# Value products of latent attention: three of nine key tiles and the value factors in fp32 instead of fp32r parts

## The chip, the cores and the metric

One core of a Trainium2 chip runs the whole kernel. The metric is device time in microseconds; the figure of a kernel is the median of its runs. The profile is of one execution of its own.

## The reference, cut to what matters

Two layers of a diffusion backbone run over 1024 latent tokens and 128 context ("prompt") tokens of width 1024. Layer 0 is multi-head latent attention with 16 heads, layer 1 a neighbourhood attention. The change is in layer 0:

```
c_kv   = rms_norm(kv_a, kv_norm_g)                       # keys x 128, shared by the heads
k_nope, v = split(c_kv @ w_kvb)                          # per head: 128 + 128
s = (q_nope @ k_nope.T + q_rope @ k_rope.T) * MLA_SCALE  # all 1024 + 128 cached context keys
o = softmax(s) @ v
y = (o * silu(gate)) @ w_out
```

The kernel doesn't form v for the latent queries. It computes (softmax(s) @ c_kv) @ w_v: a value product over the 9 key tiles of 128 keys in the latent space (tile 0 is the cached context, tiles 1 to 8 the latent tokens), and then one product with the head's 128 x 128 value factor w_v. The prompt's queries go the same way over their own 128 keys (tile 9).

## The kernel before

Precision: an fp32 operand x is split into a high part hi = fp32r(x), written by ScalarE as a copy, and a low part lo = fp32r(x - hi), written by VectorE or GpSimd (`split_to`, lines 147 to 149). A product is then three fp32r matmuls, hi*hi, hi*lo and lo*hi (`mm3`, lines 84 to 87, PASSES).

Stages: modulation, first norm, gates and narrow projections (to about 350 us); 64 units of latent attention (350 to 1203 us), a unit being one head and 256 queries; the output projection of layer 0 (to about 1500 us); layer 1.

In the attention the instructions of TensorE, ScalarE, VectorE and GpSimd are issued in an order written out by hand: ORDERS has eight strings, one for each unit modulo 8, and each engine works through its own instructions in that order. While unit `un` is finished, the scores of the next one, `nx`, are made, and the unit before, `f`, is closed. The steps:

- s0 to s4 (`scores`, line 741): scores of `nx`, two key tiles to a PSUM bank, 36 matmuls. m0 to m4 (`run_max`, lines 749 to 758): the running maximum, on ScalarE and VectorE.
- e0 to e4 (`exp`, line 799): exp of a bank of `un` to the fp32 tile `pf` (512 columns, the last 256: two key tiles of 256 queries). +1 to +4 (`sums`, lines 817 to 822): GpSimd adds the `pf` tiles up.
- h0 to h4 (`hi`, line 804, ScalarE) and l0 to l4 (`lo`, line 809, VectorE): the two parts of `pf` for the value products.
- v01, v26, v78 (`values`, line 828, booked on line 87): the value products of key tiles 0 to 1, 2 to 6 and 7 to 8, three matmuls each, summed in the bank `pso`. V (`values_out`): the result goes to `ol` as two parts, a ScalarE copy and a VectorE subtraction.
- L0 to L5 (lines 839 to 850): transpose of the sums, reciprocal, back to a row. M0 to M5 (lines 763 to 786): the same for the maxima of `nx`; M5 puts the row of maxima where X (`last_scores`, line 792) adds it to the scores in their banks. Only then can the exps of `nx` begin.
- F (`finish`, lines 854 and 856): row sums to all partitions, and the product of `ol` with the head's value factor `wv`. O (`finish_out`): gate and store.
- H takes the next of the weights' splits, P and p start a product of the next heads' queries or of the prompt (`do_prod`), ES and EV evacuate it, A runs one of its later steps, T lets it go on. The prompt's chain for two heads is in `prompt_work`; its steps `latent` and `val` are its two value products.

Banks: tag M has two PSUM banks, which `psv` (F), `pso` (first v) and `pm` (L0 and M0) take in turn. `pf` has NPF = 5 buffers, each part of it NPT = 5. The head's raw weights come by one DMA from SP's queue (`load_head`); `split_v` splits the value factor at the second unit of the head before.

```
if c == "v":
    n = step[1:]
    values(un, range(int(n[0]), int(n[-1]) + 1))
```

Of the kernel before, what the change touches and what calls it, by code (L numbers as in the profile page):

```python
# [11 lines left out]
F32 = mybir.dt.float32  # L12
# [21 lines left out]
EPS = 1e-6  # L34
GW = 64
ORDERS = [
# [8 lines left out]
]  # L45
NPF = 5
NPT = 5
NORDER = "K A0 K A1 J1 C0 Z m0 K J2 X1 W R C1 m1 X1 K K K J2 h0 x0 h1 J1 r0 l0 E R x1 l1 n0 K r1 R f n1 K K g K K"
PASSES = ((0, 0), (0, 1), (1, 0))
# [7 lines left out]
def hybrid_step(ctx: ExitStack, tc: tile.TileContext, i, o):  # L57
# [302 lines left out]
    V.tensor_copy(onesR, ones)  # L360
    cKT = [ap.tile([P, 10, P], F32R, name=f"cKT{e}") for e in range(2)]
    cK = [ap.tile([P, 10, LAT], F32R, name=f"cK{e}") for e in range(2)]
    KR = [ap.tile([P, 10, P], F32R, name=f"KR{e}") for e in range(2)]
    for j in range(10):
        V.tensor_copy(KR[1][64:66, j, :], ones[64:66, :])
# [24 lines left out]
    def narrow(t):  # L390

        j = t + 1
        ps = bank("W")[:, :NARROW]
        for ko in range(NKO):
            mm3(ps, [hT[e][:, ko, t * P:(t + 1) * P] for e in range(2)], [w448[e][:, ko, :] for e in range(2)],
                ko == 0, ko == NKO - 1)
        pj = p1.tile([P, NARROW], F32, tag="pj", name="pj", bufs=2)
        S.copy(pj, ps)
        ss = p1.tile([P, 2], F32, tag="ss2", name="ss2", bufs=2)
        junk = p1.tile([P, QLR], F32, tag="junk2", name="junk2", bufs=1)  # L400
        S.activation(junk, pj[:, 0:QLR], AF.Square, accum_out=ss[:, 0:1])
        S.activation(junk[:, :LAT], pj[:, QLR:QLR + LAT], AF.Square, accum_out=ss[:, 1:2])
        V.tensor_scalar(ss[:, 0:1], ss[:, 0:1], 1.0 / QLR, EPS, ALU.mult, ALU.add)
        V.tensor_scalar(ss[:, 1:2], ss[:, 1:2], 1.0 / LAT, EPS, ALU.mult, ALU.add)
        r = rsqrt(p1, ss, 2)

        V.tensor_scalar(pj[:, 0:QLR], pj[:, 0:QLR], r[:, 0:1], MLA_SCALE, ALU.mult, ALU.mult)
        cf = p1.tile([P, LAT], F32, tag="cf", name="cf", bufs=2)
        V.scalar_tensor_tensor(cf, pj[:, QLR:QLR + LAT], r[:, 1:2], gkv, ALU.mult, ALU.mult)
        split_to(cK[0][:, j, :], cK[1][:, j, :], cf)  # L410
        kr2 = p1.tile([P, 2, 64], F32, tag="kr2", name="kr2", bufs=2)
        krp = pj[:, QLR + LAT:NARROW]
        if t == 8:
            dma(o["s_ckv"], cf)
            dma(o["s_kr"], krp)
            V.tensor_copy(kr2[:, 0, :], krp)
        else:
            rot = p1.tile([P, 64], F32, tag="rot", name="rot", bufs=2)
            sw = krp.rearrange("p (a b c) -> p a b c", a=2, b=2)
            sv = ropeSk[:, t, :].rearrange("p (a b c) -> p a b c", a=2, b=2)  # L420
            rv = rot.rearrange("p (a b c) -> p a b c", a=2, b=2)
            for b in range(2):
                V.tensor_tensor(rv[:, :, b, :], sw[:, :, 1 - b, :], sv[:, :, b, :], ALU.mult)
            V.tensor_tensor(kr2[:, 0, :], krp, ropeCk[:, t, :], ALU.mult)
            V.tensor_tensor(kr2[:, 0, :], kr2[:, 0, :], rot, ALU.add)
        V.tensor_copy(kr2[:, 1, :], kr2[:, 0, :])
        pt = bank("T")
        nc.tensor.transpose(pt[:, 0:P], pj[:, 0:P], ident)
        nc.tensor.transpose(pt[:, P:2 * P], pj[:, P:2 * P], ident)
        nc.tensor.transpose(pt[:, 2 * P:3 * P], cf, ident)  # L430
        nc.tensor.transpose(pt[:, 3 * P:4 * P], kr2.rearrange("p a b -> p (a b)"), ident)
        qf = p1.tile([P, 2, P], F32, tag="qf", name="qf", bufs=2)
        for c in range(2):
            V.tensor_scalar(qf[:, c, :], pt[:, c * P:(c + 1) * P], gq[:, c:c + 1], None, ALU.mult)
        split_to(qaT[0][:, :, t * P:(t + 1) * P], qaT[1][:, :, t * P:(t + 1) * P], qf)
        split_to(cKT[0][:, j, :], cKT[1][:, j, :], pt[:, 2 * P:3 * P], V)
        put_kr(j, pt[:, 3 * P:4 * P])

    def load_head(h, tile_):

        raw, rr = tile_[:, 0:512], None
        dma(raw, i["whead"][h])
        if h % 2 == 0:
            rr = tile_[:, 512:768]
            dma(rr, i["wr"][h // 2].rearrange("p k c -> p (k c)"))
        return raw, rr
# [12 lines left out]
            split_to(wr[0], wr[1], rr)  # L459
        head_w[h].append(wr)  # L460

    def split_v(h, raw):
        wv = [ap2.tile([P, LAT], F32R, tag=f"wv{e}", name=f"wv{e}", bufs=4) for e in range(2)]
        split_to(wv[0], wv[1], raw[:, 384:512])
        head_wv[h] = wv

    narrow(0)
    for h in range(2, 6):
# [10 lines left out]
    for h in range(6, H - 2):  # L479
        for n, _ in enumerate(gate(h, gate_w(h))):  # L480
            for _ in range(1 + (n == 1)):
                next(rest, None)
        next(rest, None)
        if h == 10:
            raw = load_head(0, pg.tile([P, 1024], F32, tag="raw", name="w_raw", bufs=4))
            split_qk(0, raw[0])
            split_r(0, raw[1])
            split_v(0, raw[0])
    for _ in rest:
        pass  # L490
    es_m.close()
# [125 lines left out]
    def prompt_work(h):  # L617
# [43 lines left out]

        def spl(nm, n):
            def fn():
                c["t"] = [p2.tile([P, 2 * P], F32R, tag=f"{nm}{e}", name=f"{nm}{e}", bufs=1) for e in range(2)]
                split_to(c["t"][0], c["t"][1], c["s"])
                fresh.add((h, n))
            return fn

# [4 lines left out]
        def val():  # L673
            c["gt"] = p2.tile([P, 256], F32, tag="gt", name="gt", bufs=3)
            c["ps"] = bank("W")[:, :2 * P]
            for e in range(2):
                dma(c["gt"][:, e * P:(e + 1) * P], gate_d[h - 1 + e][:, qs])
                mm3(c["ps"][:, e * P:(e + 1) * P], head_wv[h - 1 + e], [x[:, e * P:(e + 1) * P] for x in c["t"]])

        def val_out(eng):  # L680
            og = p2.tile([P, 256], F32, tag="og", name="og", bufs=2)
# [140 lines left out]
            G.tensor_tensor(sm[:, 0:256], sm[:, 0:256], sm[:, 256:512], ALU.add)  # L822

    def values(un, js):
        if js[0] == 0:
            un["pso"] = bank("M")[:, :256]
        for j in js:
            mm3(un["pso"], [cK[e][:, j, :] for e in range(2)],
                [x[:, (j % 2) * 256:(j % 2) * 256 + 256] for x in un["pT"][j // 2]], j == 0, j == 8)

    def values_out(un):
        un["ol"] = [p2.tile([P, 256], F32R, tag=f"ol{e}", name=f"ol{e}", bufs=2) for e in range(2)]
        split_to(*un["ol"], un["pso"], V)

    def sum_cols(un, bank_):
        un["gt"] = load_gate(un["h"], un["qs"])
# [15 lines left out]
    def finish(un):  # L852

        nc.tensor.matmul(un["rs"][:, 0:256], onesR, row, start=True, stop=True)
        un["psv"] = bank("M")[:, :256]
        mm3(un["psv"], un["wv"], un["ol"])

    def finish_out(un):
        gr = p2.tile([P, 256], F32, tag="gr", name="gr", bufs=2)
# [28 lines left out]
    with tc.high_priority(offset=300):  # L888
# [2 lines left out]
        raw = load_head(1, pg.tile([P, 1024], F32, tag="raw", name="w_raw", bufs=4))  # L891
        split_qk(1, raw[0])
        split_r(1, None)
        split_v(1, raw[0])
    for _ in gate(H - 1, w_last, "M"):
        pass

# [98 lines left out]
    for k, (h, u) in enumerate(units):  # L996
# [13 lines left out]
        splits = deque()  # L1010
        if u == 1 and h + 1 < H:
            if h:
                splits.append(lambda: split_v(h + 1, head_raw[h + 1][0]))
            splits.append(lambda: h + 2 < H and head_raw.update({h + 2: load_head(h + 2, new_raw(0))}))
        if u == 2 and h + 2 < H:
            splits.append(lambda: split_qk(h + 2, head_raw[h + 2][0]))
# [942 lines left out]
```

## Time and profile before

| what | value |
|---|---|
| median of 3 runs | 2181.25 us |
| lowest and highest | 2176.08 and 2183.51 us |
| profiled execution, time | 2177.92 us |
| its span in the trace | 2176.1 us |
| mean granted TensorE clock | 0.98 of full speed |
| busy: TensorE, VectorE, ScalarE, GpSimd | 93%, 67%, 51%, 39% |

Times in the trace count from the start of the span. Busy is the share of the span in which an engine executes; matmuls overlap in their pipeline, so the time from start to start of neighbours tells more than the duration of one. In the timeline a row is a run of like instructions: start, length, engine, line, operation, tiles, count, and in brackets how long the engine stood idle before it and for whom. VectorE is DVE, ScalarE ACT, GpSimd POOL there; PEld is TensorE's weight load.

### The profile page before, as it was taken

The numbers are of one execution on the slowest core, as the hardware profiler recorded it, in microseconds if no ns is written. First come the engines' busy times: TensorE is split into PE (matmuls) and PEld (weight loads), VectorE is DVE, ScalarE is ACT, GpSimd is POOL, SyncE is SP. The second block draws the span as 40 slices with busy tenths as digits, with TensorE's granted clock in tenths as the row PEclk, the third lists the DMA queues.
The fourth block names the chain that finished last, engine by engine and source line by source line (L and its number), as shares of the span: only waits on it lengthen the run. The fifth ranks groups of instructions, "written<-read, shape, count | busy, mean of one in ns | idle before, by whom it ended". The sixth has DMA issues, their size and how long they took to land.

```text
span 2176.1 us, 37859 instructions
## 1 busy us (share of the span) xinstructions
PE 2017.5 (93%) x13166; PEld 1861.4 (86%) x13166; DVE 1460.2 (67%) x3224; ACT 1105.3 (51%) x2577; POOL 854.0 (39%) x847
## 2 busy tenths in 40 slices
PE   7899998889989898889898799999999999999898
PEld 3799997888888888888887788889889999999686
DVE  4723877778887888788888645642215778888743
ACT  5545115565556565656565433442214666677631
POOL 1412215676766677767665400010001333333400
PEclk9999999999999999999999999999999999999899
DMA  8223752212121212221211643425424555556753
GB/s 292 93 69 109 228 166 79 59 46 64 46 64 51 66 49 76 61 68 49 60 45 57 222 151 117 136 74 161 163 101 146 178 178 175 172 181 204 216 148 97
DMA packets 174931, 256.49 MB, mean 118 GB/s; under 512 B 20690, under 2 KB 138226, under 8 KB 174740
## 3 DMA queue, kind: packets, MB, share of 16 engines
q1 hardware_dynamic: 174476, 253.71, 37.5%
q8 instruction: 104, 1.70, 0.3%
q14 instruction: 87, 0.71, 0.1%
q10 hardware_dynamic: 136, 0.26, 0.0%
q0 software_dynamic: 128, 0.11, 0.0%
HBM read 182.58 MB, written 51.49 MB: 108 GB/s over the span
## 4 chain that ended last, share of the span: by engine, by line
PE 40%; DVE 4%; ACT 4%; POOL 4%; DMA 3%; issue 2%; SPq 0%; DVEq 0%; POOLq 0%; ACTq 0%
PE ps_S L87 16%; PE ps_W L87 11%; PE ps_M L87 5%; PE ps_M L1675 2%; POOL sm L820 2%; PE ps_T L1650 2%; PE ps_S L1623 1%; PE ps_S L1624 1%; ACT pf L799 1%; DMA vw<-vd 1%; DMA w_raw<-in_wout 1%; DVE rm L754 1%; DVE pT L809 1%; DVE og L82 1%; DMA w_raw<-og_d 1%
## 5 line engine op out<-in xcount | busy, mean ns | idle before, releaser
L809 DVE TENSOR_TENSOR pT<-pf,pT 128x512 fp32r<-128x512 f32 (+1 forms) x320 | 306.9, 963 | 24.2 <-ACT pT L804 24.0
L820 POOL TENSOR_TENSOR sm<-sm,pf 128x512 f32<-128x512 f32 (+1 forms) x192 | 259.5, 1352 | 16.0 <-ACT pf L799 2.0
L87 PE MATMUL ps_M<-pT,cK 128*128 128x256 f32 x1728 | 259.3, 296 | 1.3 <-DVE pT L809 1.3
L87 PE MATMUL ps_W<-h,w 128*128 128x384 f32 x1152 | 237.6, 345 | 0.4 <-DVE w L82 0.4
L87 PEld LDWEIGHTS ps_M<-pT,cK 128*128 128x128 f32 x1728 | 230.8, 198 | 1.9 <-DVE pT L809 1.9
L87 PEld LDWEIGHTS ps_W<-h,w 128*128 128x128 f32 x1152 | 197.9, 188 | 6.4 <-DVE w L82 0.7
L741 PE MATMUL ps_S<-qA,cKT 128*128 128x256 f32 x1152 | 190.1, 285 | 5.6 <-ACT pf L799 5.3
L87 PE MATMUL ps_S<-hT,w_hi 128*128 128x384 f32 x720 | 190.5, 342 | 4.3 <-DVE hT L82 2.6
L804 ACT CAST pT<-pf 128x512 fp32r<-128x512 f32 (+1 forms) x320 | 179.7, 591 | 0.0
L741 PEld LDWEIGHTS ps_S<-qA,cKT 128*128 128x128 f32 x1152 | 166.2, 192 | 8.2 <-ACT pf L799 7.6
L1645 POOL TENSOR_SCALAR pf<-pf,li 128x512 f32<-128x512 f32 x128 | 90.7, 709 | 199.3 <-DVE li L1642 176.7
L87 PEld LDWEIGHTS ps_S<-hT,w_hi 128*128 128x128 f32 x720 | 130.9, 189 | 6.7 <-DVE hT L82 3.3
L817 POOL TENSOR_TENSOR sm<-pf 128x512 f32<-128x512 f32 x64 | 88.8, 1387 | 110.7 <-ACT pf L799 110.4
L87 PE MATMUL ps_S<-wo,og 128*128 128x512 f32 x432 | 124.0, 395 | 0.0
L786 ACT CAST q<-ps_M 2x256 fp32r<-2x256 f32 x63 | 22.7, 360 | 197.3 <-PE ps_M L780 185.1
L87 PE MATMUL ps_S<-hT,w_lo 128*128 128x384 f32 x360 | 121.8, 339 | 0.0
L1639 ACT ACTIVATE pf<-pf,nm 128x512 f32<-128x512 f32 x128 | 93.0, 726 | 34.0 <-DVE nm L1636 30.8
L741 PE MATMUL ps_S<-q,KR 128*128 128x256 f32 x384 | 108.6, 284 | 0.3 <-DMA q<-w_raw 0.3
L799 ACT ACTIVATE pf<-ps_S 128x512 f32<-128x512 f32 x192 | 108.8, 598 | 0.0
L82 DVE TENSOR_TENSOR og<-w_raw,og 128x512 fp32r<-128x512 f32 x56 | 57.0, 1038 | 67.4 <-ACT og L148 54.2
L519 ACT COPY qt<-ps_W 128x384 f32<-128x384 f32 (+1 forms) x104 | 46.9, 451 | 100.3 <-PE ps_W L87 93.2
L741 PE MATMUL ps_T<-qA,cKT 128*128 128x256 f32 x576 | 97.2, 284 | 0.0
(376 smaller groups left out, 5035.4 us busy)
## 6 DMA issues: line engine op xcount, KB each, us to landing
w_raw<-in_w_ada SPq DMA_DIRECT2D x48, 512.0 KB
w_raw<-og_d SPq DMA_DIRECT2D x41, 512.0 KB
vw<-vd SPq DMA_DIRECT2D x128, 128.0 KB
bias<-in_bias SPq DMA_DIRECT2D x64, 192.0 KB
q<-rp SPq DMA_DIRECT2D x126, 96.0 KB
gate_d<-gt SPq DMA_DIRECT2D x48, 192.0 KB
w_raw<-in_wgate SPq DMA_DIRECT2D x16, 512.0 KB
gt<-gate_d SPq DMA_DIRECT2D x64, 128.0 KB
```

What stands on the lines that cost most here:

```text
L82: eng.tensor_tensor(out, a, b, ALU.subtract)
L87: nc.tensor.matmul(ps, lhs[a], rhs[b], start=first and n == 0, stop=last and n == 2)
L519: (eng.copy if eng is S else eng.tensor_copy)(out, src)
L741: nc.tensor.matmul(ps[:, c:c + 256], k_[:, j, :], q_[:, un["qs"]], start=c == 0 and n == 0, stop=n == 3, skip_group_check=True)
L799: S.activation(pf, un["banks"][b][:, :w], AF.Exp)
L804: S.copy(un["pT"][b][0][:, :pf.shape[1]], pf)
L809: V.tensor_tensor(x[1], pf, x[0].bitcast(F32), ALU.subtract)
L817: G.tensor_tensor(un["sm"], un["pf"][0], pf, ALU.add)
L820: G.tensor_tensor(sm[:, :w], sm[:, :w], pf, ALU.add)
L1639: S.activation(it["pf", rg], it["pf", rg], AF.Exp, bias=it["nm", rg], scale=1.0, accum_out=it["li", rg])
L1645: G.tensor_scalar(it["pf", rg], it["pf", rg], it["li", rg][:, 0:1], 1.0, ALU.mult, ALU.mult)
L1650: nc.tensor.transpose(pt[:, j * P:(j + 1) * P], it["pf", rg][:, j * P:(j + 1) * P], ident)
```

## The change

Key tiles 6, 7 and 8 (from WHOLE = 6 on) are kept as plain fp32 in `cKf` and multiplied with the plain `pf` tiles 3 and 4, one fp32 matmul instruction for three fp32r ones. The steps h3, h4, l3 and l4 go from all eight orders. The value products change their order: v68 (fp32) stands first, at or behind the place of v01 and behind e4, then v03 in the place of v26, then v45 in that of v78. The value factor `wv` isn't split: it has a DMA of its own and is multiplied in fp32 with an unsplit `ol`, in F and in the prompt's `val`; `values_out` is one ScalarE copy. The prompt's last split (`spl("tp", 3)`) becomes a ScalarE copy alone.

```diff
 ORDERS = [
...
-    "H e0 F s0 H O e1 T +1 h0 s1 l0 e2 A m0 m1 h1 e3 s2 +2 P +3 s3 l1 m2 h2 l2 h3 e4 ES h4 m3 v01 s4 +4 A A m4 P L0 M0 l3 A A M1 L1 A L2 A M2 p v26 L3 M3 ES L4 w l4 A EV M4 ES A v78 M5 V L5 X",
+    "H e0 F s0 H O e1 T +1 h0 s1 l0 e2 A m0 m1 h1 e3 s2 +2 P +3 s3 l1 m2 h2 l2 e4 ES m3 v68 s4 +4 A A m4 P L0 M0 A A M1 L1 A L2 A M2 p v03 L3 M3 ES L4 w A EV M4 ES A v45 M5 V L5 X",
...
-    "F e0 O H ES s0 H e1 +1 h0 s1 l0 T e2 A m0 e3 m1 s2 p m2 T e4 h1 +2 +3 s3 l1 h2 l2 h3 m3 p +4 s4 m4 v01 h4 ES l3 P M0 P L0 L1 M1 L2 v26 M2 L3 ES A M3 l4 w L4 M4 v78 A M5 L5 X V",
+    "F e0 O H ES s0 H e1 +1 h0 s1 l0 T e2 A m0 e3 m1 s2 p m2 T e4 h1 +2 +3 s3 l1 h2 l2 m3 p +4 s4 m4 v68 ES P M0 P L0 L1 M1 L2 v03 M2 L3 ES A M3 w L4 M4 v45 A M5 L5 X V",
...
 NPF = 5
+WHOLE = 6
...
+    cKf = ap.tile([P, 9 - WHOLE, LAT], F32, name="cKf")
...
-        cf = p1.tile([P, LAT], F32, tag="cf", name="cf", bufs=2)
+        cf = cKf[:, j - WHOLE, :] if WHOLE <= j < 9 else p1.tile([P, LAT], F32, tag="cf", name="cf", bufs=2)
         V.scalar_tensor_tensor(cf, pj[:, QLR:QLR + LAT], r[:, 1:2], gkv, ALU.mult, ALU.mult)
-        split_to(cK[0][:, j, :], cK[1][:, j, :], cf)
+        if not WHOLE <= j < 9:
+            split_to(cK[0][:, j, :], cK[1][:, j, :], cf)
...
-        dma(raw, i["whead"][h])
+        dma(raw[:, 0:384], i["whead"][h][:, 0:384])
...
-    def split_v(h, raw):
-        wv = [ap2.tile([P, LAT], F32R, tag=f"wv{e}", name=f"wv{e}", bufs=4) for e in range(2)]
-        split_to(wv[0], wv[1], raw[:, 384:512])
-        head_wv[h] = wv
+    def load_v(h):
+        head_wv[h] = ap2.tile([P, LAT], F32, tag="wv", name="wv", bufs=4)
+        dma(head_wv[h], i["whead"][h][:, 384:512])
...
-                mm3(c["ps"][:, e * P:(e + 1) * P], head_wv[h - 1 + e], [x[:, e * P:(e + 1) * P] for x in c["t"]])
+                nc.tensor.matmul(c["ps"][:, e * P:(e + 1) * P], head_wv[h - 1 + e],
+                                 c["t"][0][:, e * P:(e + 1) * P].bitcast(F32), start=True, stop=True)
...
     def values(un, js):
-        if js[0] == 0:
+        if js[0] == WHOLE:
             un["pso"] = bank("M")[:, :256]
         for j in js:
-            mm3(un["pso"], [cK[e][:, j, :] for e in range(2)],
-                [x[:, (j % 2) * 256:(j % 2) * 256 + 256] for x in un["pT"][j // 2]], j == 0, j == 8)
+            c = slice((j % 2) * 256, (j % 2) * 256 + 256)
+            if j >= WHOLE:
+                nc.tensor.matmul(un["pso"], cKf[:, j - WHOLE, :], un["pf"][j // 2][:, c], start=j == WHOLE, stop=False)
+            else:
+                mm3(un["pso"], [cK[e][:, j, :] for e in range(2)], [x[:, c] for x in un["pT"][j // 2]], False,
+                    j == WHOLE - 1)
 
     def values_out(un):
-        un["ol"] = [p2.tile([P, 256], F32R, tag=f"ol{e}", name=f"ol{e}", bufs=2) for e in range(2)]
-        split_to(*un["ol"], un["pso"], V)
+        un["ol"] = p2.tile([P, 256], F32, tag="ol", name="ol", bufs=2)
+        S.copy(un["ol"], un["pso"])
...
-        mm3(un["psv"], un["wv"], un["ol"])
+        nc.tensor.matmul(un["psv"], un["wv"], un["ol"], start=True, stop=True)
...
-                splits.append(lambda: split_v(h + 1, head_raw[h + 1][0]))
+                splits.append(lambda: load_v(h + 1))
```

## Rows read from the trace of the kernel before

**Rows 1.** Busy time by engine in the attention's stretch (us, instructions; clock, DMA).

```profile
350.00:1203.00 853.00, 765.93 (x6017) 732.56 (x6017) 697.87 (x1388) 503.08 (x1181) 579.92 (x495) 0.98 0.20 57
```

**Rows 2.** Waits, 350 to 1203 us: total us, times, longest.

```profile
ACT q L786 <- PE ps_M L780: 185.1, 58, 7.7
...
PE ps_M L763 <- DVE rm L758: 37.5, 30, 3.3
PE ps_M L839 <- POOL sm L820: 35.4, 49, 2.1
```

**Rows 3.** Timeline of TensorE: waits at L0 and M0.

```profile
675.88 0.44 PE L839 MATMUL ps_M<-ident,sm 128*128 128x128 f32 x2 [0.84 <-POOL sm L820]
...
700.78 0.44 PE L839 MATMUL ps_M<-ident,sm 128*128 128x128 f32 x2 [0.49 <-POOL sm L820]
701.67 0.44 PE L763 MATMUL ps_M<-ident,rm 128*128 128x128 f32 x2 [0.45 <-DVE rm L758]
...
713.55 0.44 PE L839 MATMUL ps_M<-ident,sm 128*128 128x128 f32 x2 [0.34 <-POOL sm L820]
...
725.75 0.44 PE L839 MATMUL ps_M<-ident,sm 128*128 128x128 f32 x2 [0.47 <-POOL sm L820]
...
740.57 0.44 PE L763 MATMUL ps_M<-ident,rm 128*128 128x128 f32 x2 [1.33 <-DVE rm L758]
...
755.52 0.44 PE L763 MATMUL ps_M<-ident,rm 128*128 128x128 f32 x2 [3.08 <-DVE rm L758]
...
770.10 0.44 PE L763 MATMUL ps_M<-ident,rm 128*128 128x128 f32 x2 [0.69 <-DVE rm L758]
...
545.16 0.44 PE L763 MATMUL ps_M<-ident,rm 128*128 128x128 f32 x2 [1.82 <-DVE rm L758]
```

**Rows 4.** Timeline of TensorE, value products of one unit and their neighbours.

```profile
710.81 0.87 PE L87 MATMUL ps_M<-pT,cK 128*128 128x256 f32 x6
711.52 0.52 PE L741 MATMUL ps_T<-qA,cKT 128*128 128x256 f32 x3
...
713.96 2.04 PE L87 MATMUL ps_M<-pT,cK 128*128 128x256 f32 x15
...
715.85 0.28 PE L780 MATMUL ps_M<-identR,lir 128*2 128x128 f32 x2
```

**Rows 5.** Timeline of line 179, then single tiles: duration in ns (least/median/most), forms.

```profile
25.41 1.88 PE L179 MATMUL ps_S<-w_raw,c 128*4 128x512 f32 x4
27.22 0.63 PE L179 MATMUL ps_S<-w_hi,cs 128*4 128x512 f32 x2
...
L179 PEld LDWEIGHTS ps_S<-w_raw,c x16: 82/86/87, 25.4 to 38.3; 128*4 128x4 f32 x16
...
L190 PEld LDWEIGHTS ps_T<-sel,mod x32: 181/187/187, 23.3 to 42.0; 5*128 5x128 f32 x32
...
L87 PEld LDWEIGHTS ps_M<-pT,cK x1728: 186/188/338, 352.0 to 1199.7; 128*128 128x128 f32 x192
```

**Rows 6.** Groups by line and form, VectorE: count, busy us, mean ns, idle before.

```profile
L809 DVE TENSOR_TENSOR pT<-pf,pT 128x512 fp32r<-128x512 f32 x256 | 279.3, 1096 | 24.2 <-ACT pT L804 24.0
...
L82 DVE TENSOR_TENSOR ol<-ps_M,ol 128x256 fp32r<-128x256 f32 x64 | 27.1, 423 | 78.7 <-ACT ol L148 78.6
```

**Rows 7.** Timeline behind the 3.08 us gap; windows with the granted clock (third from last).

```profile
756.02 3.47 PE L87 MATMUL ps_M<-pT,cK 128*128 128x256 f32 x15
759.33 0.28 PE L780 MATMUL ps_M<-identR,lir 128*2 128x128 f32 x2
...
545.00:549.00 4.00, 3.84 (x34) 3.81 (x35) 3.32 (x13) 1.08 (x4) 1.40 (x2) 1.00 0.00 0
756.00:758.00 2.00, 2.00 (x11) 2.00 (x10) 1.62 (x9) 0.00 (x0) 0.00 (x0) 0.50 0.00 0
```

**Rows 8.** Timeline of VectorE: l3 and the last part of the maxima.

```profile
713.35 0.70 DVE L809 TENSOR_TENSOR pT<-pf,pT 128x512 fp32r<-128x512 f32 x1
...
715.51 0.15 DVE L775 TENSOR_TENSOR nmr<-nm,nmr 128x2 fp32r<-128x2 f32 x1
```

More of the change, by code (lines that the diff above doesn't have):

```diff
@@ L487, in hybrid_step @@
             split_r(0, raw[1])
-            split_v(0, raw[0])
+            load_v(0)
     for _ in rest:
@@ L663, in fn @@
             def fn():
-                c["t"] = [p2.tile([P, 2 * P], F32R, tag=f"{nm}{e}", name=f"{nm}{e}", bufs=1) for e in range(2)]
-                split_to(c["t"][0], c["t"][1], c["s"])
+                c["t"] = [p2.tile([P, 2 * P], F32R, tag=f"{nm}{e}", name=f"{nm}{e}", bufs=1) for e in range(4 - n)]
+                if n == 3:
+                    S.copy(c["t"][0].bitcast(F32), c["s"])
+                else:
+                    split_to(c["t"][0], c["t"][1], c["s"])
                 fresh.add((h, n))
@@ L824, in values @@
     def values(un, js):
-        if js[0] == 0:
+        if js[0] == WHOLE:
             un["pso"] = bank("M")[:, :256]
         for j in js:
-            mm3(un["pso"], [cK[e][:, j, :] for e in range(2)],
-                [x[:, (j % 2) * 256:(j % 2) * 256 + 256] for x in un["pT"][j // 2]], j == 0, j == 8)
+            c = slice((j % 2) * 256, (j % 2) * 256 + 256)
+            if j >= WHOLE:
+                nc.tensor.matmul(un["pso"], cKf[:, j - WHOLE, :], un["pf"][j // 2][:, c], start=j == WHOLE, stop=False)
+            else:
+                mm3(un["pso"], [cK[e][:, j, :] for e in range(2)], [x[:, c] for x in un["pT"][j // 2]], False,
+                    j == WHOLE - 1)
     def values_out(un):
-        un["ol"] = [p2.tile([P, 256], F32R, tag=f"ol{e}", name=f"ol{e}", bufs=2) for e in range(2)]
-        split_to(*un["ol"], un["pso"], V)
+        un["ol"] = p2.tile([P, 256], F32, tag="ol", name="ol", bufs=2)
+        S.copy(un["ol"], un["pso"])
     def sum_cols(un, bank_):
@@ L893, in hybrid_step @@
         split_r(1, None)
-        split_v(1, raw[0])
+        load_v(1)
     for _ in gate(H - 1, w_last, "M"):
```

12 rows, old and new, of the table ORDERS are left out of this document.

## The prediction, made before the result

> **What bounds the kernel now.** I read the page first, then the busy time by stretch, the waits of the latent attention, and last the timeline of single units. The change lives in the 64 units of latent attention (a head and 256 queries each), from 350 to 1203 us of the span. TensorE is busy for 766 of those 853 us, VectorE for 698, GpSimd for 580, ScalarE for 503 [rows 1]. So TensorE is nearest to its limit, but not at it: about 13.3 us pass per unit, and it stands still in one place above all, at L0 and M0, the transposes of the sums (line 839) and of the maxima (line 763). It waits there 35 us for GpSimd's sums and 38 us for VectorE's running maximum [rows 2]. ScalarE stands 185 us before the copy of line 786, waiting for TensorE [rows 2]: time freed on ScalarE alone falls into that idle time.
>
> The gaps at L0 and M0 repeat every eight units (eight orders in ORDERS). One round, from 675 us on, reads, gaps of one unit added: 0.84 (the next unit is alike at 0.8, one row stands for both), 0.49+0.45, 0.34, 0.47, then 1.33, 3.08 and 0.69 for the maximum [rows 3]; before the 1.33 and the 0.69 stands also a wait for GpSimd of at least the size of the 0.34. Order 6 has the 3.08.
>
> A unit is therefore a loop: last scores (line 792), exps, GpSimd's chain of sums and VectorE's of maxima, L0 and M0, then the products that cover the small steps M1 to M5, then the next unit's last scores. Work put ahead of L0 is free as far as it fills the gap; work taken away behind M0 shortens the loop, until the small steps are what is late.
>
> **What the change costs on TensorE.** A value product of one key tile is today three fp32r matmuls of 256 columns: the six of v01 take 711.52-710.81 = 0.71 us [rows 4], 0.12 each, 0.36 for three. No fp32 matmul with a 128 x 128 weight and 256 columns stands in this trace. The nearest are those of line 179: eight fp32 products left 16 weight loads and 16 matmul records, two each, and four records in a row take 27.22-25.41 = 1.81 us, 0.45 each, for 512 columns [rows 5]. 512 columns at 2.4 GHz are 0.213 us, so a record streams its columns twice (0.427) and at most 0.026 is extra. With 256 columns a record is 0.213 to 0.239 and a product 0.43 to 0.48 us; I take 0.45, the middle. So fp32 costs 0.09 us more for each triple: three key tiles and the product with the value factor make 0.37 per unit, 24 us over 64 units, if nothing hides it.
>
> The weight load could spoil this. Line 190 loads 128 fp32 columns in 187 ns; the fp32r loads of the value products take 188 [rows 5]. Both exceed 0.12 us and the fp32r ones are hidden in a stream of 0.12 per matmul, so I take the fp32 ones as hidden under 0.21; exposed, they would add up to 0.187-0.082 = 0.105 per record (0.082 is a load of four columns) [rows 5]. The Trainium skill (TensorE: Matmul & The Clock Gate, Weight-path perf modes) says that a fast weight load is on for 128 columns unless the input is FP32. By that rule the new products could lose a fast load that the old ones have, and the sum would be that of rival B; by the two loads of equal length there is nothing to lose.
>
> **Where it lands.** The order matters more than the 24 us. Ahead of L0 stood v01, 0.71; there now stands v68, 3 x 0.45 = 1.35, +0.64. The finish of the unit before (F, ahead of all scores) grows by 0.09. Insert ahead of L0: 0.73 us (0.65 to 0.85 with the two prices). Where the last wait is for the maximum, VectorE's chain also starts 0.09 later, as its step O waits for F. Against the gaps of [rows 3], L0 or M0 come later by 0, 0, 0.09, 0.73-0.34 = 0.39, 0.73-0.47 = 0.26, 0.09, 0.09, 0.09: 1.0 us per round of eight. v68 reads only the exps 3 and 4, no parts; the last scores' banks are refilled by steps s3 and s4, which wait for the same exps anyway, so no new wait arises. The rotation of the two M banks (psv, pso, pm) keeps its order, and psv's bank comes free earlier, as values_out is one copy.
>
> Behind M0 stood v26, 15 matmuls, 715.85-713.96 = 1.89 us; v03 has 12, so 0.36 less is on the path. v45 replaces v78 at 0.71 for 0.71. Can M1 to M3 follow? In the unit at 713 us VectorE has the last part at 715.51+0.15 = 715.66, and M4's work starts at 715.85 [rows 4, 8]: 0.19 of the 0.36 is won, then VectorE is late. That holds in the four units where M0 follows L0 at once without a wait for the maximum. In the other four L1 is done while M0 waits, and l3, a 0.70 us step that sits ahead of M1 in VectorE's queue [rows 8], is gone; there I count all 0.36. Per round 4 x 0.19 + 4 x 0.36 = 2.2 us. Net -1.2 per round, -9.5 for eight rounds.
>
> **The clock.** After the gap of 3.08 us, v26 takes 759.33-756.02 = 3.31 us instead of 1.89 (its 15 records end when the next group starts; the row gives 3.47 with the last one's tail); the granted clock there is 0.50, the 1.2 GHz level [rows 7]. That repeats in six of the eight rounds, with gaps from 3.0 to 3.3; after 1.82 us at 545 the clock stayed at 1.00 [rows 3, 7]. With the insert the gap becomes 3.08+0.09-0.73 = 2.4, between the two. I count half of six falls as avoided: 3 x 1.42 = 4.3 us.
>
> **What costs or gives nothing.** l3 and l4, h3 and h4, and the lower part of ol leave. A full-width l is 1.10 us on the mean, the lower part of ol 0.42 [rows 6], so VectorE loses some 2 us per unit. But l3 begins after the maximum's last step (713.35 against m4 ahead of it) and ol's part is done in F's cover, so the chain to M0 is not shortened; only l3's place ahead of M1 is, counted above. If that cover were gone (VectorE itself the bound), it would be worth up to 2 us per unit. wv's split leaves ScalarE and GpSimd once a head, the prompts' lower part once per head pair; they make sums earlier where the insert already fills the gap: 0. The value factor has its own DMA, one more issue per head on SP's queue, ahead of the next head's weights and gates; it is read three units later, and the list of waits over this stage names no DMA among its longest. The prompt's value products (two fp32 of 128 columns for six fp32r) cost at most 2 x 0.45 - 6 x 0.12 = +0.18 per head pair and give at most about 0.5: 0. Key tiles 6 to 8 lose a split each in the projection, outside the loop: 0.
>
> Sum: -9.5 - 4.3 = -13.8. The profiled execution took 2177.92 us, 2176.1 of them the span; 3.3 below the median of 2181.25. So 2164 by the profile's own time, **2167 us** against the median.
>
> **Rivals.**
> A, no change: the small steps, not the products, end behind M0. If the four adjacent units win nothing and the others 0.19, a round nets 1.0-0.76 = +0.25, +2 in all, and with the clock's 4.3 the time is 2179. For it: only 0.19 us separates VectorE's last part from M4. Against: l3 leaves that queue.
> B, slower: fp32 weight loads are exposed. A product is then 0.45+0.21 = 0.66; the insert 3 x 0.66 - 0.71 + 0.30 = 1.57, F's shift 0.30. L0 or M0 shift by 0.73, 0.78, 0.63, 1.23, 1.10, 0.30, 0.30, 0.54: 5.6, less 2.2, x 8 = +27; the 3.08 gap shrinks to the 1.8 that kept the clock, -8.5. About 2200. It decides from a product of some 0.55 us on, where shifts (2.8) eat the gain and the clock's share. Against: the loads of [rows 5].
> C, more gain: v03's 0.36 is won in all eight units (1.0-2.9 = -1.9, -15) and all six falls go (-8.5): 2158. Further below if GpSimd's sums get shorter too. The Trainium skill (SBUF — State Buffer, Who interferes with whom) says that a VectorE instruction with two SBUF inputs contends with GpSimd's reads; l3 and l4 are such, and by that the sums could gain, a time near 2150. The rows speak against: l3 stands behind the maxima, when the sums are nearly through.
>
> **How the numbers follow.** Forecast 0.55, A 0.21, B 0.14, C 0.10. A difference under 0.3% (6.5 us) can hardly be told from none here. The forecast's own range is 2158 to 2176; a little of it is within 0.3%. Faster: 0.55+0.10 less 0.03 = 0.62; same 0.21+0.03 = 0.24; slower 0.14. The range reaches past C's 2158 and A's 2179 by about the scatter of the runs shown (2176 to 2184), some 6 us: 2152 to 2186, leaving out B and the tails.
>
> **What would show it.** In the changed profile: fp32 records of 256 columns at 0.21 to 0.24 us from start to start, two per product; gaps at L0 gone in units with 0.3 to 0.8 before; about 2.4 us left in order 6's unit, with fewer stretches at half clock behind it; 0.2 to 0.4 us less from M0 to the last scores. Wrong it would be if the records take more than 0.27, if M4 waits for VectorE or the last scores for line 786's copy, or if the maxima come earlier than now.

## The result, and the profile after

The changed kernel takes 2154.03 us (median of four runs, 2150.59 to 2155.87), the kernel before 2182.38 in four. The ratio is 0.9873, with an interval of 0.9848 to 0.9898: 28 us less, where 14 were forecast. 2154 is inside the range of 2152 to 2186 and just below the forecast's own, 2158 to 2176. The profiled span falls from 2176.1 to 2150.7 us.

Busy time of the changed kernel in the attention's stretch, in the columns of [rows 1], and below it the waits of TensorE's matmuls there (us in total, times, longest):

```profile
350.00:1180.00 830.00, 774.24 (x5767) 727.22 (x5766) 608.48 (x1197) 456.75 (x1042) 555.66 (x473) 0.99 0.21 59
```

```profile
PE ps_M L769 <- DVE rm L764: 29.3, 31, 1.8
...
PE ps_M L786 <- DVE lir L781: 10.9, 17, 1.9
...
PE ps_M L849 <- POOL sm L826: 7.7, 13, 1.6
```

The whole gain is here: from the second of the 64 last-scores steps to the last, the attention takes 830.4 us before and 804.2 after, 26.2 less. TensorE's busy time in these rows is 8 us longer, but it stands still far less. L0's wait for GpSimd's sums is down from 35.4 to 7.7 us and M0's wait for the maximum from 37.5 to 29.3 [rows 2]. A wait that was short grew: M4 waits 10.9 us for VectorE's parts. Before, that was 4.7:

```profile
PE ps_M L780 <- DVE lir L775: 4.7, 6, 1.6
```

The end of a unit in order 5 and of the unit in order 6 behind it, on TensorE (start, length, engine, line, operation, tiles, count, idle before):

```profile
730.10 1.46 PE L836 MATMUL ps_M<-pf,cKf 128*128 128x256 f32 x6
731.20 1.40 PE L88 MATMUL ps_W<-qaT,wr 128*128 128x384 f32 x6
732.44 0.38 PE L849 MATMUL ps_M<-ident,sm 128*128 128x128 f32 x2
734.09 0.44 PE L769 MATMUL ps_M<-ident,rm 128*128 128x128 f32 x2 [1.27 <-DVE rm L764]
734.28 1.67 PE L88 MATMUL ps_M<-pT,cK 128*128 128x256 f32 x12
735.83 0.28 PE L786 MATMUL ps_M<-identR,lir 128*2 128x128 f32 x2
...
748.07 0.44 PE L769 MATMUL ps_M<-ident,rm 128*128 128x128 f32 x2 [1.78 <-DVE rm L764]
...
748.48 1.67 PE L88 MATMUL ps_M<-pT,cK 128*128 128x256 f32 x12
750.03 0.28 PE L786 MATMUL ps_M<-identR,lir 128*2 128x128 f32 x2
```

The three fp32 products of v68 are six records at line 836. L0 follows in order 5 without a wait. M0 still waits, but in order 6 for 1.78 us where [rows 3] had 3.08, and v03 behind it runs at full clock: 750.03-748.48 = 1.55 us for 12 matmuls, where [rows 7] had 3.31 for 15. The window over it shows a granted clock of 1.00 (third from last), the 2.4 GHz level:

```profile
748.40:750.10 1.70, 1.70 (x17) 1.61 (x15) 1.30 (x7) 0.00 (x0) 0.00 (x0) 1.00 0.00 0
```

**Where a round gains.** A round of eight units takes 105.9 us before and 101.9 after (640 to 750 us of both traces). Read unit by unit from last scores to last scores, ahead of M0's start the round is 1.25 shorter: order 5 by 0.59, order 6 by 0.68, order 1 by 0.15, while orders 3 and 4 lose 0.11 and 0.02 (order 3's L0 itself starts 0.17 later). Behind M0 it is 1.27 shorter without the clock, and 1.5 more come from the full clock in order 6. Over the whole stretch the second value step (v26, v03) was longer than its usual length (2.04 and 1.68 us) by a quarter microsecond or more in eight units before, 9.8 us together, and in one after, 1.2 (counted behind 410 us).

### The profile page after: what moved, and what is told of

It is laid out like the page before. It is cut to its first block, busy times and chain, and to the rows that moved or that the text cites. A ratio compares the mean times of both kernels' runs of the same rounds, so it can differ in the third digit from the quotient of the medians.

```text
span 2150.7 us, 36948 instructions
## 1 busy us (share of the span) xinstructions
PE 2027.4 (94%) x12894; PEld 1857.6 (86%) x12894; DVE 1371.6 (64%) x3032; ACT 1057.4 (49%) x2430; POOL 821.9 (38%) x820
## 5 line engine op out<-in xcount | busy, mean ns | idle before, releaser
L815 DVE TENSOR_TENSOR pT<-pf,pT 128x512 fp32r<-128x512 f32 x192 | 231.2, 1212 | 40.5 <-ACT pT L810 40.2
L747 PE MATMUL ps_S<-qA,cKT 128*128 128x256 f32 x1152 | 202.8, 296 | 4.1 <-ACT pf L805 3.9
L747 PEld LDWEIGHTS ps_S<-qA,cKT 128*128 128x128 f32 x1152 | 171.8, 193 | 10.6 <-ACT pf L805 6.3
L88 PE MATMUL ps_M<-pT,cK 128*128 128x256 f32 x1152 | 168.1, 290 | 0.0
L88 PEld LDWEIGHTS ps_M<-pT,cK 128*128 128x128 f32 x1152 | 146.5, 190 | 0.0
L810 ACT CAST pT<-pf 128x512 fp32r<-128x512 f32 x192 | 118.9, 631 | 0.0
L747 PE MATMUL ps_T<-qA,cKT 128*128 128x256 f32 x576 | 101.7, 292 | 0.0
```

What stands on the lines that cost most here:

```text
L88: nc.tensor.matmul(ps, lhs[a], rhs[b], start=first and n == 0, stop=last and n == 2)
L747: nc.tensor.matmul(ps[:, c:c + 256], k_[:, j, :], q_[:, un["qs"]], start=c == 0 and n == 0, stop=n == 3, skip_group_check=True)
L810: S.copy(un["pT"][b][0][:, :pf.shape[1]], pf)
L815: V.tensor_tensor(x[1], pf, x[0].bitcast(F32), ALU.subtract)
```

## The experiments

The ratios are to the kernel before, with a 95% interval. Each kernel ran beside the kernel before on one chip; the chips differ, and the median of the kernel before was 2177.72 to 2182.38 us on them, so ratios can be compared across groups of runs and times only within one. The stretch is the attention from the second last-scores step to the last, in the profile. The slow steps are the second value steps behind 410 us that are lengthened by over a quarter microsecond, and their excess together.

| kernel | ratio | stretch, us | slow steps, us |
|---|---|---|---|
| before | 1 | 830.4 | 8, 9.8 |
| changed | 0.9873 [0.9848, 0.9898] | 804.2 | 1, 1.2 |
| order_only | 0.9923 [0.9898, 0.9947] | 818.0 | 1, 0.4 |
| fp32_last | 0.9989 [0.9976, 1.0003] | 825.5 | 3, 3.0 |
| tiles_only | 0.9891 [0.9867, 0.9914] | 809.3 | 3, 2.9 |
| factor_only | 0.9976 [0.9962, 0.9990] | 820.8 | 6, 6.6 |
| idle_splits | 0.9943 [0.9926, 0.9961] | 815.9 | 5, 4.0 |
| one_input | 0.9962 [0.9947, 0.9977] | 814.7 | 5, 4.8 |
| act_copies | 0.9874 [0.9859, 0.9889] | 800.4 | 1, 0.4 |
| five_tiles | 0.9783 [0.9764, 0.9802] | 780.8 | none |
| after_again | 0.9865 [0.9848, 0.9882] | 802.2 | 1, 1.1 |
| copies_again | 0.9863 [0.9846, 0.9881] | 800.3 | 1, 0.4 |
| five_copies | 0.9746 [0.9729, 0.9763] | 776.9 | none |
| seven_tiles | 0.9724 [0.9708, 0.9740] | 772.0 | none |

**order_only: only work moved ahead of L0, all of it in parts as before.**

```diff
-... v01 ... L0 M0 ... v26 ... v78
+... v02 ... L0 M0 ... v36 ... v78
```

In the third order v02 stands behind e4 and h2, as v68 does in the change.

> The kernel before, all nine tiles and the factor still in parts; only the order of the value products moves: tiles 0 to 2 ahead of L0 and M0 (behind h2 in the third order), 3 to 6 behind, 7 to 8 last. Theory 'place': three products that fill the gaps at L0 and shorten the way from M0 to the last scores carry the gain, so most of it stays: about 2165 (0.36 us less behind M0 where VectorE keeps up, 1 to 2 us per round, and some of the stretches at half clock gone). Rival 'relief': VectorE's fewer splits carry it, and the order alone is worth nothing: 2180, within 0.3% of before.

Measured 2163.93 us. Place alone is worth 12.4 us of the stretch, and most of it is the clock: the slow steps fall from 9.8 to 0.4 us. Over the whole stretch the time at the lower clock falls from 37.5 to 20.5 us, which is worth half the difference, 8.5 us, if TensorE works throughout: two thirds of the 12.4. The wait at L0 shrinks, but a new one comes: tile 2 needs VectorE's step l1, and v02 waits for it. In order 6 that cuts the long wait in two:

```profile
PE ps_M L839 <- POOL sm L820: 13.5, 20, 1.7
PE ps_M L87 <- DVE pT L809: 8.1, 12, 0.8
```

```profile
747.10 0.50 PE L87 MATMUL ps_M<-pT,cK 128*128 128x256 f32 x2 [0.83 <-DVE pT L809]
...
749.83 0.44 PE L763 MATMUL ps_M<-ident,rm 128*128 128x128 f32 x2 [1.19 <-DVE rm L758]
```

The fp32 tiles of the change need no parts and have no such wait.

**fp32_last: the changed kernel with its fp32 tiles at the end.**

```diff
-... v68 ... L0 M0 ... v03 ... v45
+... v01 ... L0 M0 ... v25 ... v68
```

> The changed kernel with its value products in the old order of tiles: 0 to 1 ahead of L0, 2 to 5 behind M0, the three fp32 tiles last. All splits stay removed. 'Place': behind M0 now stand 1.43 + 1.30 us where the changed kernel has 1.43 + 0.71, so each unit loses some 0.6 us there and the gaps at L0 come back by 0.6; the gain is nearly gone: 2175 to 2185. 'Relief': the gain stays within 8 us of the changed kernel: 2155 to 2162.

Measured 2176.54 us, no difference that can be told. The same arithmetic gives nothing where it stands last. The wait at L0 is back (the row below), and from M0 to the last scores the way is longer than in the kernel before, by 0.2 us in orders 3, 4 and 7 and by less in 0, 1 and 5:

```profile
PE ps_M L848 <- POOL sm L826: 29.3, 44, 1.7
```

**tiles_only and factor_only: the two halves of the change.** The first keeps the value factor, `ol` and the prompt's last split in parts. The second is the kernel before with this, the same in the prompt's chain, and the factor's own DMA:

```diff
-        split_to(*un["ol"], un["pso"], V)
+        S.copy(un["ol"], un["pso"])
...
-        mm3(un["psv"], un["wv"], un["ol"])
+        nc.tensor.matmul(un["psv"], un["wv"], un["ol"], start=True, stop=True)
```

> The changed kernel, but the value factor and ol split into parts as before (F three fp32r products, one VectorE subtraction and two splits per head back); cK has only the seven slots it needs. Both theories leave most of the gain here: 2155 to 2163. If it is the removed split of the factor (ScalarE and GpSimd work ahead of the sums, once a head) that matters, half the gain goes: 2168.

> The kernel before with only the value factor and ol unsplit (own DMA, one fp32 product in F and in the prompt). 'Place' and 'relief' of the tiles' splits: no change beyond 0.3%: 2176 to 2186, slightly later F (0.07 us) against an earlier start of the sums in the two units of a round that lose the split. If the factor carries the gain: below 2170.

Measured 2157.86 and 2173.81 us. The tiles carry the change. The factor, expected to give nothing, gives a little (0.24%). One product is longer, while VectorE loses the lower part of `ol`, and ScalarE and GpSimd lose the factor's split; which of these gives the gain was not separated.

**idle_splits: the changed kernel with h3, h4, l3 and l4 back in their places, their results read by nobody.**

```diff
-... m4 v68 ES P M0 P L0 L1 M1 L2 v03 M2 L3 ES A M3 w L4 M4 v45 ...
+... m4 v68 h4 ES l3 P M0 P L0 L1 M1 L2 v03 M2 L3 ES A M3 l4 w L4 M4 v45 ...
```

> The changed kernel with h3, h4, l3 and l4 put back in their old places in all eight orders; their parts are written and not read. All that the tiles' splits give by leaving (the relief of ScalarE and VectorE) is gone, fp32 products and order stay. If order alone carries the gain: 2154 to 2159, like the changed kernel. If relief has a share: near the run with the order alone, 2160 to 2168.

Measured 2162.43 us: of the changed kernel's 1.3% only 0.57% is left, and the stretch is 11.7 us longer than with the splits gone. Its waits show where:

```profile
PE ps_M L769 <- DVE rm L764: 31.3, 30, 2.1
PE ps_M L786 <- DVE lir L781: 15.0, 23, 2.2
PE ps_M L849 <- POOL sm L826: 10.1, 15, 1.6
```

Against the changed kernel these are 2.0, 4.1 and 2.4 us more, 8.5 of the 11.7. The time at the lower clock is 20.5 us against 17.1, worth 1.7 more by the same count. That leaves some 1.5 open. So the relief works on all three waits, not at one place. The run puts back ScalarE's copies and VectorE's subtractions together and doesn't say which matters. The profiled execution took 2170.97 us, the longest of its six, so its figures may be high.

Place and relief need each other: with the splits kept, the new place gives 0.57% (idle_splits) or 0.77% (order_only); with the splits gone and the tiles in the old order nothing can be told (fp32_last); with both it is 1.27%.

**one_input: factor_only with one step of the maxima made a reduction.** In factor_only, as before, the step that merges the two halves of the running maximum (both in SBUF) takes 0.42 us in most units and 1.18 in some. The edit gives it one input:

```diff
-            V.tensor_tensor(m, m, rm[:, 256:512], ALU.max)
+            un["rm2"] = p2a.tile([P, 256], F32, tag="rm2", name="rm2", bufs=1)
+            V.tensor_reduce(un["rm2"], rm.rearrange("p (a b) -> p b a", a=2), AX.X, ALU.max)
...
-            V.tensor_tensor(m, ps[:, 0:256], m, ALU.max)
+            V.tensor_tensor(m, ps[:, 0:256], un["rm2"], ALU.max)
```

> The kernel before with the factor in fp32 (2174 in the call before), and VectorE's step of the maxima that merges two halves of rm in SBUF written as a reduction with one input to a new tile. Theory 'port': in orders 5 and 6 that step takes 1.18 us instead of 0.42, since GpSimd's lower part of qA starts in front of it and VectorE's second SBUF input waits for GpSimd; with one input (some 0.6 us expected) M0 comes 0.5 us earlier in both, some 8 us in all, 2163 to 2168, more if stretches at half clock go too. Rival: the step is slow for another reason, or M0 is held by something else: 2171 to 2177.

Measured 2167.88 us. The step has one length in all 64 units (least, median, most, in ns):

```profile
L760 DVE TENSOR_REDUCE rm<-rm x64: 691/696/716, 336.9 to 1164.4; 128x256 f32<-128x512 f32 x64
```

It is slower than 0.42 and never 1.18, though 14 of the 64 start while a GpSimd instruction runs. In order 6, M0 comes 0.46 to 0.50 us earlier in the four rounds in which factor_only's merge took 1.18, as expected. In two rounds in which it took 0.43, M0 comes 0.28 later, and in order 7 0.2 to 0.3 later: without a clash the reduction only costs. So of the stretch's 6.1 us only 1.1 are waits for the maximum; the wait for the sums fell by more, from 31.3 to 24.5, and why is open. The interval overlaps factor_only's. The edit thus shows that the long form goes with the two-input merge; that its removal shortens the whole kernel is not resolved by the times. The operation and the output tile changed along with the number of inputs.

**act_copies: the changed kernel with the upper parts of L2 and M2 on ScalarE in orders 1 and 3.**

```diff
-        V.tensor_copy(r[:, 0::2], un[src])
+        copy_by(eng or V, r[:, 0::2], un[src])
```

with `eng` ScalarE in those two orders.

> The changed kernel with steps L2 and M2 (copies of two columns) on ScalarE in orders 1 and 3, where VectorE's copy took 0.65 and 0.70 us instead of 0.16 beside GpSimd's lower part of qA and TensorE then waited 0.37 and 0.55 us for the parts. 'Port': those waits go, up to 0.9 us per round, 2147 to 2151. Rival: the copies are late for another reason, or ScalarE's copies and the hand-over cost as much: 2153 to 2157.

**five_tiles: tiles 4 and 5 in fp32 too, h2 and l2 gone.** Order of the value steps as in the change; v45 is now fp32. The strings of the orders, the slots of `cK` and the start and stop flags follow.

```diff
-WHOLE = 6
+WHOLE = 4
```

> The changed kernel with key tiles 4 and 5 in fp32 too (h2 and l2 gone, v45 at its place in fp32 from pf 2; cK with five slots). TensorE gets 2 x 0.08 us more per unit behind M0, +10 us over 64 units; VectorE loses a full-width l of 1.2 us ahead of the maxima's last steps. If VectorE's maxima still hold M0 in orders 5, 6, 7 and 0 (waits of 1.3, 1.8, 0.6 and 0.2 in the changed kernel), up to 3 us per round come back against 1.3 lost: 2138 to 2148. If the waits stay for another reason: 2160 to 2168.

Measured together: act_copies 2148.49 and five_tiles 2127.57 us, the latter some 10 us below what was expected. The first looked like 3 to 5 us against the changed kernel's time on another chip, though the ratios are alike (0.9874 and 0.9873), so it was run beside the changed kernel itself, with the combination and one step further (WHOLE = 2, h1 and l1 gone too; only tiles 0 and 1 are left in parts):

> The changed kernel once more, beside the others on one chip: 2150 to 2156.

> The changed kernel with L2 and M2 on ScalarE in orders 1 and 3, to be compared in one call. 'Port': 3 to 5 us below the changed kernel (the waits for the parts fell from 0.37 and 0.55 us to nearly nothing in the profile of the first such run, 0.5 us per round). Rival: no difference beyond 2 us.

> Five fp32 tiles and the ScalarE copies in orders 1 and 3 together. Five tiles alone took 2128, and left 12 us of waits for the parts in 17 places: 3 to 6 us less, 2122 to 2125, if the two add up.

> Seven of nine tiles in fp32 (2 to 8; h1 and l1 gone as well). In the run with five tiles VectorE's maxima hold M0 for 8 us in all, GpSimd's sums for 6. If TensorE is the bound from there, two more tiles add 0.15 us per unit, 10 us, and save at most 8: 2128 to 2138. If relief still pays (VectorE's l1 stands beside GpSimd's sums and both get shorter): below 2125.

after_again took 2150.05 and copies_again 2150.06 us: the copies' move removes a wait (M4's total, 11.0 us in after_again, is 5.3), the stretch is 1.9 us shorter, and the times show nothing. With five tiles the same move may give 0.4% (0.9746 against 0.9783, the intervals barely apart, on two chips). five_copies took 2123.54, seven_tiles 2119.05 us, the fastest kernel here: not the 2128 to 2138 of a bound TensorE but the other branch, in which relief still pays. All nine tiles in fp32 was not tried. In seven_tiles' attention TensorE is busy for 776 of 800 us, VectorE for 491, and M0 no longer waits:

```profile
350.00:1150.00 800.00, 776.31 (x5529) 724.80 (x5528) 491.25 (x1065) 391.10 (x911) 505.13 (x470) 1.00 0.22 62
```

```profile
PE ps_M L769 <- DVE rm L764: 0.4, 1, 0.4
```

TensorE's busy time hardly moved: within the stretch it is 751 us in both kernels, of 804.2 in the changed one and of 772.0 here. What goes is the standing still.

## Why the prediction was right in sign and short by half

**The fp32 product: right, at its low end.** The six records of v68 take 731.20-730.10 = 1.10 us to the next group's start, and that group's 1.40 instead of 1.20 holds 0.20 more of them: 1.30, or 0.217 per record and 0.433 per product, against 0.45 taken. That is four times 0.107 us, the streaming of 256 columns at 2.4 GHz. The Trainium skill (FP8 and Floating Point Precision, TensorE Precision Notes) counts four passes for true fp32; the trace agrees. Rival B needed exposed loads. They are as long as the fp32r ones of [rows 5], and the stream hides them:

```profile
L836 PEld LDWEIGHTS ps_M<-pf,cKf x384: 187/190/193, 352.5 to 1168.3; 128*128 128x128 f32 x192
```

The Trainium skill's rule that fast weight load excludes FP32 (TensorE: Matmul & The Clock Gate, Weight-path perf modes) has no loss to show here.

**The insert ahead of L0: over-priced.** Predicted were L0 or M0 later by 1.0 us per round; in orders 3 and 4, for which 0.39 and 0.26 were counted, it is 0.17 and 0.02. One cause lies in the reading. Ends of matmuls are modelled, and a group that waits for nothing starts before the end of the one ahead:

```profile
706.49 1.23 PE L88 MATMUL ps_W<-qaT,wa 128*128 128x384 f32 x6
707.56 0.38 PE L849 MATMUL ps_M<-ident,sm 128*128 128x128 f32 x2
```

706.49+1.23 = 707.72, and L0 starts at 707.56. An idle time in brackets, counted from the modelled end, so hides 0.16 us more slack than it says. The insert itself was 3 x 0.433 - 0.71 + 0.07 = 0.66 instead of 0.73. The two make up 0.23 us, which is the whole miss in orders 3 and 4.

**"The chain to M0 is not shortened" is the step that failed.** It spoke of l3, l4 and `ol` as work behind or beside the maxima. But in orders 5 and 6, the units with the longest waits, the maxima came earlier, which the prediction had named as a sign of being wrong. In the kernel before, VectorE and GpSimd in order 6:

```profile
647.70 0.98 POOL L82 TENSOR_TENSOR qA<-qt,qA 128x384 fp32r<-128x384 f32 x1
...
647.79 1.18 DVE L756 TENSOR_TENSOR rm<-rm 128x256 f32<-128x256 f32 x1
649.08 0.42 DVE L758 TENSOR_TENSOR rm<-ps_T,rm 128x256 f32<-128x256 f32 x1
```

and in the changed kernel:

```profile
645.14 0.43 DVE L762 TENSOR_TENSOR rm<-rm 128x256 f32<-128x256 f32 x1
645.47 1.00 POOL L83 TENSOR_TENSOR qA<-qt,qA 128x384 fp32r<-128x384 f32 x1 [0.38 <-ACT qA L149]
645.67 0.42 DVE L764 TENSOR_TENSOR rm<-ps_T,rm 128x256 f32<-128x256 f32 x1
```

GpSimd's subtraction for qA started 0.09 us ahead of the merge, and the merge took 1.18 us; where it starts 0.33 behind, the merge takes 0.43. The 0.75 saved is order 6's gain of 0.68 ahead of M0, with the longer F against it. Over the 64 units the merge takes more than 0.7 us in 15 before, in 4 after. In the trace before, these 15 and no others start while a GpSimd instruction runs, and each ends 0.28 us behind the end of that one; the other 49 take 0.42 or 0.43, though in 40 of them a GpSimd instruction starts. The step behind the merge, the same maximum with one input in PSUM, takes 0.41 to 0.43 in all 64, 43 of which start while GpSimd works. The Trainium skill (SBUF — State Buffer, Who interferes with whom) says that a VectorE instruction with two SBUF inputs contends with a GpSimd instruction that reads SBUF, that issue order decides who blocks, and that on this chip a reduction never contends; the 15 and 49 merges here and one_input's 691 to 716 ns agree.

Which edit removes the clash differs by order. In order 6 it is gone with the new order alone (order_only) and stays in four of eight rounds of factor_only. In order 5 the merge is still 1.2 us in most rounds of order_only, tiles_only, factor_only and idle_splits, and is 0.51 us in five of eight rounds only where both the splits and the parts of `ol` and `wv` are gone (changed, fp32_last). So it is a matter of which of two engines is a tenth or two ahead, and not a gain that an edit owns: this part of the 28 us is luck. In five_tiles and seven_tiles long merges are back, in 27 and 22 units, while M0's whole wait for the maximum is 8.2 and 0.4 us. Rival C named this port rule for the sums. It acted on the maxima.

**Behind M0: the term was too large.** 2.2 per round were predicted, 1.27 came. Orders 1 and 3 got longer there, by 0.13 and 0.35. The predicted sign of error, M4 waiting for VectorE, is in the trace, in the unit at 707 us:

```profile
709.19 0.70 DVE L777 CAST lir<-li 128x2 fp32r<-128x2 f32 x1
709.80 0.15 DVE L777 CAST nmr<-nm 128x2 fp32r<-128x2 f32 x1
```

```profile
708.86 1.00 POOL L83 TENSOR_TENSOR qA<-qt,qA 128x384 fp32r<-128x384 f32 x1 [1.51 <-ACT qA L149]
```

```profile
710.14 0.28 PE L786 MATMUL ps_M<-identR,lir 128*2 128x128 f32 x2 [0.55 <-DVE lir L781]
```

A copy of two columns that takes 0.15 alone takes 0.70 when it starts while GpSimd works on qA, and M4 waits 0.55. All 14 such copies of over 0.3 us in the changed kernel start beside a running GpSimd instruction and end 0.02 to 0.03 us behind its end. They have one input, so two inputs in SBUF are not the only form that waits. act_copies took the wait away without a measurable gain: most of the slack won there was lost elsewhere, and where is left open.

**The clock: right mechanism, half the size.** The forecast saw the gap of order 6 shrink to 2.4 us and counted half of six falls, 4.3 us. Insert and earlier maxima together made it 1.78, and 8.6 us came back. order_only, with none of the relief, avoids the falls of order 6 too, with the wait cut into 0.83 and 1.19 us. By the granted clock over the whole stretch, 37.5 us at the lower level before and 17.1 after, the clock's part comes to 10.2 us if TensorE works throughout, near the 8.6.

**The sum.** Predicted for eight rounds: +8 ahead of M0, -17.6 behind it, -4.3 for the clock. Measured: -10.0, -10.2 and -8.6, 28.8 in all by the typical round and 26.2 over the stretch. The term ahead of M0 was wrong by 18 us, of which some 7 are the over-priced insert (0.8 per round) some 10 the earlier maxima (1.27 per round in orders 5 and 6), and some 1 order 1, 0.15 per round. That last one is at L0, and factor_only has it alone (0.16): there the sums do come earlier by the unsplit factor, which the prediction had put at 0.

## What to carry to other kernels

Where an engine waits for several chains at the loop's head, put the work that needs the least preparation there: the same fp32 products gave nothing at the end of the unit and over 1% ahead of the wait. Two key tiles in plain fp32 cost 2 x 0.08 us more than in fp32r parts, and took a ScalarE copy and a VectorE subtraction of 1.10 us on the mean [rows 6] off engines that were late; go on with the trade while TensorE still stands still. Before you write "this engine's relief doesn't shorten the chain", list the chain's instructions with their longest durations, not their medians, and see what ran beside the long ones.

## What the runs showed of the hardware

- Two of VectorE's instructions have two lengths: 0.42 and 1.18 us for a merge of 128x256 with both inputs in SBUF, 0.15 and 0.70 for a copy of two columns. The long ones started while a GpSimd instruction was under way and ended just behind it, 0.28 and 0.02 to 0.03 us. Ninety nanoseconds in the start decided it. A maximum with one input in PSUM (0.42) and a reduction with one input (0.69) kept their length.
- Some two thirds of what a mere reordering gained (8.5 of 12.4 us, by half of the time saved at the lower level) was the granted clock: after each of six waits of 3.0 to 3.3 us at M0 the value step behind it was lengthened as in [rows 7], where the granted clock is at the 1.2 GHz level. After the 1.2 to 1.8 us of the same units in the changed kernel it was not; after 1.9 to 2.1 in idle_splits it was, in part, in four of seven units. One unit of the changed kernel, in order 5, was lengthened after waits of 0.78 at L0 and 1.33 at M0, so the length of one wait does not decide it alone.
